# Two chunks per matmul in the last two doubling steps of a block inverse

## The chip, the cores and the metric

The kernel runs on one core of a Trainium2 chip. Its engines work side by side, each through its own instructions in order: TensorE (PE, the matmuls; the loads of its stationary operand are shown apart as PEld), VectorE (DVE), ScalarE (ACT), GpSimd (POOL), and SyncE (SP), which issues the DMAs. The metric is the time of one execution on the device in microseconds (us); less is better.

## What is computed

One inference step of a hybrid decoder layer for a prompt of 2048 tokens and for eight single tokens: a mixer (convolution heads beside gated DeltaNet heads), attention into a memory, and a feed-forward network. The part that matters here is the gated DeltaNet of the prompt, four heads (H) with keys and values of 128 elements. Cut to what matters, the reference says:

```
decay = exp(where(incl, gc[..., :, None] - gc[..., None, :], -inf))
kb = k * beta[..., None]
lower = where(strict, einsum('nbhid,nbhjd->nbhij', kb, k) * decay, 0.0)
a_mat = lower + eye(c)
u = triangular_solve(a_mat, v * beta[..., None], lower=True, unit_diagonal=True)
w = triangular_solve(a_mat, kb * exp(gc)[..., None], lower=True, unit_diagonal=True)
```

For each chunk of tokens a matrix with ones on its diagonal and entries only below it has to be inverted, or a system with it solved. The chunks are then passed through in order, each updating a state of 128x128.

## The kernel before

The kernel takes chunks of 128 tokens (P) and works on blocks of 512 tokens (TB), so a block has four chunks (NT = 4), and there are four blocks (NB). For each block and each head, 16 times in all, `dn_front` (L1810) prepares the four chunks together; `dn_chain` (L1966) then carries the state through them.

`dn_front` is a generator. It builds `lt` (L1822, L1875), the transposed strictly triangular matrices of the four chunks side by side, 128 partitions by 4 x 128. It inverts the 16x16 blocks on the diagonal with small operations of VectorE and GpSimd in `base_inverse` (L1771), whose scratch is the tile `bit` (L1893). The small inverses go through DRAM into two tiles: `Tm` (L1913), the inverse so far, and `W` (L1910), its transpose. Then the inverse is doubled three times, from blocks of 16 to 32, 32 to 64 and 64 to 128 (L1927 to L1961). One doubling fills the off-diagonal block of each pair of finished blocks: the product of the entry below the diagonal with one finished block (`pu1`, result in `u1`, negated), and the product of the other finished block with that (`pu2`). For each of the two products there is one float32 matmul per chunk, four in all. In the first two doublings VectorE multiplies the first product by a mask of -1 and 0 (`nms`, L2114), so that only the wanted blocks stay, and adds the second to `Tm`. Then TensorE transposes `Tm` (`ptw`) and ScalarE copies the result into a new tile `W`. In the third doubling the operands have 64 columns or 64 rows, ScalarE takes both results out of PSUM, and the second goes straight into `W`. At its end `dn_front` hands `W` on.

In profiles the tiles go by their names without numbers: `pu1` and `pu2` both as `pu`, `u1` as `u`. Every instruction has the line L530, where the planner issues it.

The order of the work is planned in two passes. The generators are lanes of `Sched` (L561): the main program emits the projections (`hd`, `glua`, `glub`, then `rg`, `sc`, `fx`, `fy`, `fz`, `dn`), and after each group of matmuls `tick` (L597) lets every lane whose wait is due by a rough clock emit its next operations. All operations go onto a `Tape` (L155). Its `order` (L316) then simulates the five engines with a cost for each operation (L189) and latencies between engines (L159), takes on each engine the ready operation with the lowest key, and so fixes the order in which each engine gets its instructions. It can also move an elementwise operation between VectorE and GpSimd. Operands of the projections are split in two parts (`w`, in float32r) by ScalarE, VectorE and GpSimd.

The tiles of 512 columns come from a pool of 28 (`t2`, L712). A lane asks for room before it takes one. Only one front at a time is in the doublings (`held_l`, L1920), and a front waits for the one before it (L1915).

Of the kernel before, what the change touches and what calls it, by code (L numbers as in the profile page):

```python
# [10 lines left out]
AF = mybir.ActivationFunctionType  # L11
ALU = mybir.AluOpType
AX = mybir.AxisListType

P = 128
# [5 lines left out]
NT = TB // P  # L21
# [91 lines left out]
def elems(ap):  # L113
    n = 1
    for x in ap.shape[1:]:
        n *= x
    return n
# [530 lines left out]
def bc(ap, axis, shape):  # L648
    return ap.unsqueeze(axis).broadcast_to(shape)
# [3 lines left out]
def hybrid_step(ctx: ExitStack, tc: tile.TileContext, i: dict, o: list):  # L653
# [4 lines left out]
    GS, PE, SP = tape.port(nc.gpsimd, "pool"), tape.port(nc.tensor, "pe"), tape.port(nc.sync, "sp")  # L658
    V, A, G = Engine(tape.port(nc.vector, "dve"), "dve", C), Engine(tape.port(nc.scalar, "act"), "act", C), Engine(GS, "pool", C)
    S = Sched(C)  # L660

    def dma(out, in_, after=0.0):
        SP.dma_start(out=out, in_=in_)
        n = 4
        for x in out.shape:
            n *= x
        C.at["sp"] = max(C.at["sp"] + 60, C.when([in_]), after)
        C.at["dma"] = max(C.at["dma"], C.at["sp"] + 1100) + max(n / 360.0, 60.0)
        C.ready[out.name] = max(C.ready.get(out.name, 0.0), C.at["dma"] + 1650)
        C.used[in_.name] = max(C.used.get(in_.name, 0.0), C.at["dma"])  # L670

    def mm(out, lhsT, rhs, start, stop, skip=False):
        n = elems(rhs)
        four = lhsT.dtype == F32 or n < 256
        S.wait(max(C.when([lhsT, rhs]), C.ready.get("free " + out.name, 0.0) if start else 0.0))
        PE.matmul(out, lhsT, rhs, start=start, stop=stop, skip_group_check=skip)
        C.run("pe", 3 + max(n, 64) * (4 if four else 1) / 2.4, [lhsT, rhs], out, 90.0)
# [9 lines left out]
    def transpose(out, in_, identity):  # L687
        S.wait(max(C.when([in_]), C.ready.get("free " + out.name, 0.0)))
        PE.transpose(out, in_, identity)
        C.run("pe", 110.0, [in_], out, 90.0)  # L690
# [14 lines left out]
    def nm(s):  # L705
        uid[0] += 1
        return f"{s}_{uid[0]}"
# [4 lines left out]
    def t2(name, shape=(P, TB), dt=F32):  # L712
        n = 1
        for x in shape[1:]:
            n *= x
        t = t2pool.tile([P, W2], dt, tag="t2", name=nm(name))
        live["t2"].add(t.name)
        assert len(live["t2"]) <= NT2, sorted(live["t2"])
        v = t[: shape[0], :n]
        if len(shape) == 3:  # L720
            v = v.rearrange("p (a b) -> p a b", a=shape[1])
        return v
# [7 lines left out]
    def drop(*tiles):  # L730

        for t in tiles:
            kind = "t2" if t.name in live["t2"] else "act"
            live[kind].remove(t.name)
# [4 lines left out]
    def ps(name, tag="s", shape=(P, TB)):  # L739
        n = 1  # L740
        for x in shape[1:]:
            n *= x
        t = psum.tile([P, 512], F32, tag=tag, name=nm(name), bufs=C.nbank[tag])
        v = t[: shape[0], :n]
        at = C.bank_free(tag)
        C.ready["free " + v.name] = 0.0 if at == float("inf") else at
        C.ring.setdefault(tag, []).append(v.name)
        if len(shape) == 3:
            v = v.rearrange("p (a b) -> p a b", a=shape[1])
        elif len(shape) == 4:  # L750
            v = v.rearrange("p (a b c) -> p a b c", a=shape[1], b=shape[2])
        return v

    def small(name, shape, tag=None, bufs=None, dt=F32):
        return sm.tile(list(shape), dt, tag=tag or name, name=nm(name), bufs=bufs)

    def const(name, shape, dt=F32):
        return cst.tile(list(shape), dt, tag=name, name=name)
# [994 lines left out]
    def z_full(z):  # L1753

        f = z.rearrange("a b -> (a b)").rearrange("(c x) -> c x", c=NT)
        return f[:, 0 : P * P].rearrange("c (r i) -> r c i", i=P)

    def z_diag(z):

        return z[:, 0:2048].rearrange("p (j i) -> p j i", i=P)[:, :, 0:16]  # L1760

    def z_odd(z):

        f = z.rearrange("a b -> (a b)").rearrange("(c x) -> c x", c=NT)
        return f[:, 0 : 64 * P].rearrange("c (r i) -> r c i", i=P)
# [39 lines left out]
    def left(x, s, odd=0):  # L1805
        return x.rearrange("p c (b e s) -> p c b e s", e=2, s=s)[:, :, :, odd, :]

    held_x, held_w, held_l = [], [], []

    def dn_front(h, b, sc, prev, out):  # L1810
# [11 lines left out]
        du, lt = (t2(k, (P, NT, P)) for k in ("du", "lt"))  # L1822
# [19 lines left out]
        for c in range(NT):  # L1842
            V.scalar_tensor_tensor(
                out=du[:, c, :], in0=rb[:, c, :], scalar=gcol[:, c : c + 1], in1=mneg, op0=ALU.subtract, op1=ALU.add
# [30 lines left out]
        for c in range(NT):  # L1875
            V.scalar_tensor_tensor(
                out=lt[:, c, :], in0=pkk[:, c, :], scalar=brk[:, c : c + 1], in1=du[:, c, :], op0=ALU.mult, op1=ALU.mult
# [11 lines left out]
        for c in range(NT):  # L1889
            mm(pqk[:, c, :], kT[:, cs(c)], qT[:, cs(c)], True, True)  # L1890
        V.tensor_tensor(out=at, in0=pqk, in1=du, op=ALU.mult)
        drop(qT, vT)
        bit = t2("bit", (32, 512))  # L1893
        out["pre"] = True
        yield x16

# [6 lines left out]
            out=t16.rearrange("p (i j) -> p i j", j=16), in_=w16[:, 0:256].rearrange("p (j i) -> p i j", i=16), func=AF.Copy  # L1903
        )
        dma(z_odd_diag(zw[z]), w16[1:32:2, 0:256].rearrange("p (j i) -> p j i", i=16))
        dma(z_diag(zt_[z]), t16.rearrange("p (j i) -> p j i", i=16))
        drop(bit, du)
        held_x.pop()
        held_w.pop()
        W = t2("W", (P, NT, P))  # L1910
        GS.memset(W[64:P], 0.0)
        dma(W[0:64], z_odd(zw[z]))
        Tm = t2("Tm", (P, NT, P))  # L1913
        dma(Tm, z_full(zt_[z]))
        yield lambda: prev is None or "done" in prev  # L1915
        yield [Tm, lt, W]

        u1 = u1s[0]
# [3 lines left out]
        lo = small("lo", [P, NT, 64], bufs=1)  # L1922
# [1 line left out]
        yield lo  # L1924


        for s in LEV[:-1]:  # L1927
            n = nms[s].shape[0]
            yield ("ps", "s")
            pu = ps("pu1", shape=(n, NT, 64))  # L1930
            for c in range(NT):
                mm(pu[:, c, :], (lo if n == 64 else lt)[:, c, :], left(Tm, s)[:, c], True, True)
            V.tensor_tensor(out=u1[:n], in0=pu, in1=bc(nms[s], 1, [n, NT, 64]), op=ALU.mult)
            yield u1
            yield ("ps", "s")
            pu = ps("pu2", shape=(P, NT, 64))
            for c in range(NT):
                mm(pu[:, c, :], W[:, c, :], u1[:, c, :], True, True)
            V.tensor_tensor(out=left(Tm, s), in0=pu.rearrange("p c (b s) -> p c b s", s=s), in1=left(Tm, s), op=ALU.add)
            yield Tm  # L1940
            yield ("ps", "s")
            pt = ps("ptw", shape=(P, NT, P))
            for c in range(NT):
                transpose(pt[:, c, :], Tm[:, c, :], ident)
            drop(W)
            W = t2("W", (P, NT, P))
            A.activation(out=W, in_=pt, func=AF.Copy)
            yield W

        held_l.pop()  # L1950
        yield ("ps", "s")
        pu = ps("pu1", shape=(P, NT, 64))
        for c in range(NT):
            mm(pu[64:P, c, :], lt[:, c, 64:P], Tm[:, c, 0:64], True, True)
        A.activation(out=u1[64:P], in_=pu[64:P], func=AF.Copy, scale=-1.0)
        yield u1
        yield ("ps", "s")
        pu = ps("pu2", shape=(64, NT, 64))
        for c in range(NT):
            mm(pu[:, c, :], u1[64:P, c, :], W[64:P, c, 64:P], True, True)  # L1960
        A.activation(out=W[0:64, :, 64:P], in_=pu, func=AF.Copy)  # L1961
        yield W
        drop(lt, Tm)
        out.update(kd=kd, vn=vn, W=W, at=at, qg=qg, kT=kT, s12=s12, brk=brk, held=held, done=True)
# [146 lines left out]
    mneg = const("mneg", [P, P])  # L2111
    GS.memset(mneg, 0.0)
    GS.affine_select(out=mneg, in_=mneg, compare_op=ALU.is_ge, fill=-1e30, base=0, pattern=[[1, P]], channel_multiplier=-1)
    LEV = (16, 32, 64)  # L2114
    nms = {}
    for s, n_ in ((16, 64), (32, P)):
        m = const(f"nms{s}", [n_, 64])
        GS.memset(m, -1.0)
        nb, w_ = 64 // s, n_ // 64 * s
        GS.affine_select(out=m, in_=m, compare_op=ALU.is_ge, fill=0.0, base=s - w_, pattern=[[-w_, nb], [0, s]], channel_multiplier=1)  # L2120
        GS.affine_select(out=m, in_=m, compare_op=ALU.is_ge, fill=0.0, base=w_ - 1, pattern=[[w_, nb], [0, s]], channel_multiplier=-1)
        nms[s] = m
    A.activation(out=nea, in_=nea, func=AF.Exp)
    V.tensor_scalar(out=nea, in0=nea, scalar1=-1.0, scalar2=None, op0=ALU.mult)

# [118 lines left out]
    for pair in PAIRS:  # L2244
# [3 lines left out]
        for st in STEPS:  # L2248
# [49 lines left out]
            if st[0] == "h":  # L2298
                for b in pair:
                    S.add(dn_front(k, b, scs_[b], before(fr_, b, k), fr_[b, k]), SLACK)  # L2300
                    chains.append(S.add(dn_chain(k, b, fr_[b, k], scs_[b], before(ch_, b, k), ch_[b, k]), SLACK))
# [52 lines left out]
    for dh in range(2):  # L2354
        for hp in range(2):
            wts = [ws.get("w_mqT", "r", e, dh * TB) for e in range(4 * hp, 4 * hp + 4)]
            for k in range(4):
                pt = pm("wk")
                for hh in range(2):
                    for c in range(2):  # L2360
                        w_ = wts[2 * hh + c]
# [32 lines left out]
    def square_gemm(w, src, order, xs, done, dec, apart):  # L2394
# [45 lines left out]
        out=sel2, in_=ident.rearrange("p (j c) -> p c j", j=4)[:, 0:DEC, :], op=ALU.add, axis=AX.X  # L2440
# [707 lines left out]
```

## Time and profile before

| | us |
|---|---|
| median of 3 runs | 2921.02 |
| lowest, highest | 2919.77, 2921.06 |
| the profiled execution | 2920.37 |
| its span, first to last instruction | 2918.7 |

The profile is of one execution. It shows for each engine how long it was busy, and groups instructions by engine, operation and tiles; a row of a group ends with its busy time, the mean duration of one instruction in ns, and the idle time of the engine just before them. A table of stretches gives busy time and the number of instructions of each engine between two times, counted from the start of the span. The timeline merges neighbouring instructions of one form; its columns are start, length, engine, line, operation, tiles, form and count. As matmuls overlap, the length of a group there reaches into the next group.

### The profile page before, as it was taken

How to read it: one execution, taken by the hardware profiler on the slowest of the kernel's cores; microseconds unless marked ns; L12 is line 12 of the kernel's file. 1: busy time of each engine (PE TensorE's matmuls, PEld its weight loads, DVE VectorE, ACT ScalarE, POOL GpSimd, SP SyncE). 2: the span in 40 equal slices, each digit the busy share in tenths (PEclk: the TensorE clock that was granted, in tenths of full speed). 3: DMA queues.
4: the chain of work that ended last, by engine and by line, in shares of the span. 5: the costliest groups of instructions: out<-in, count | busy, mean ns of one | idle time of the engine just before them, and what ended most of it. 6: DMA issues, size and time to landing. Idle time of an engine off the chain costs nothing.

```text
span 2918.7 us, 55833 instructions
## 1 busy us (share of the span) xinstructions
PE 2880.8 (99%) x19620; PEld 2599.1 (89%) x19620; DVE 2477.8 (85%) x5383; ACT 1447.7 (50%) x3031; POOL 749.6 (26%) x848
## 2 busy tenths in 40 slices
PE   9999999999989999999999999999999999999998
PEld 7999878888878887999988789999888999999998
DVE  8768998999969977988888977888867888888888
ACT  7544555555764445555555444444444444444444
POOL 3211243443513024622201710000532232400000
PEclk9999999999999999999999999999999999999999
DMA  6433334778764434766677767777626666666664
GB/s 220 146 105 106 119 122 144 235 252 263 231 236 126 124 102 124 258 183 224 209 257 258 257 218 253 244 231 241 201 87 222 208 214 192 210 232 193 214 212 130
DMA packets 363033, 569.41 MB, mean 195 GB/s; under 512 B 55840, under 2 KB 158560, under 8 KB 362736
## 3 DMA queue, kind: packets, MB, share of 16 engines
q1 hardware_dynamic: 362752, 565.84, 60.3%
q8 instruction: 155, 2.54, 0.3%
q14 instruction: 126, 1.03, 0.1%
HBM read 457.77 MB, written 108.51 MB: 194 GB/s over the span
## 4 chain that ended last, share of the span: by engine, by line
PE 86%; DVE 7%; DMA 4%; issue 2%; ACT 1%; POOL 1%; SPq 0%; POOLq 0%; DVEq 0%; ACTq 0%
PE hd L530 12%; PE fy L530 11%; PE rg L530 11%; PE fz L530 8%; PE fx L530 7%; PE dn L530 6%; PE dx L530 5%; PE sc L530 5%; PE glub L530 3%; PE glua L530 3%; PE dz L530 3%; PE pu L530 2%; DVE cacc L530 2%; PE mkv L530 1%; PE dy L530 1%
## 5 line engine op out<-in xcount | busy, mean ns | idle before, releaser
L530 ACT ACTIVATE w<-raw 128x512 fp32r<-128x512 f32 (+1 forms) x1066 | 649.2, 619 | 898.4 <-PE dx L530 131.1
L530 DVE TENSOR_TENSOR w<-raw,w 128x512 fp32r<-128x512 f32 (+1 forms) x866 | 609.1, 708 | 157.3 <-ACT w L530 145.8
L530 PE MATMUL fy<-op,w 128*128 128x256 f32 (+1 forms) x3168 | 434.8, 282 | 0.9 <-DMA w<-sums 0.7
L530 PEld LDWEIGHTS fy<-op,w 128*128 128x128 f32 x3168 | 399.3, 188 | 6.7 <-DVE ffs L530 2.2
L530 PE MATMUL hd<-hT,w 128*128 128x512 f32 (+2 forms) x1920 | 395.6, 356 | 1.3 <-ACT w L530 1.2
L530 POOL TENSOR_TENSOR w<-raw,w 128x512 fp32r<-128x512 f32 (+1 forms) x200 | 281.2, 1412 | 372.7 <-ACT w L530 323.0
L530 DVE SCALAR_TENSOR_TENSOR cacc<-cu,cw,cacc 128x512 f32<-128x512 f32 x480 | 358.7, 747 | 8.6 <-ACT cacc L530 4.8
L530 PEld LDWEIGHTS hd<-hT,w 128*128 128x128 f32 x1920 | 302.4, 188 | 45.8 <-ACT w L530 1.8
L530 PE MATMUL fx<-op,w 128*128 128x256 f32 (+1 forms) x2112 | 297.2, 283 | 0.3 <-ACT ffs L530 0.2
L530 PE MATMUL fz<-op,w 128*128 128x256 f32 (+1 forms) x2112 | 285.0, 282 | 1.7 <-DMA w<-sums 1.0
L530 PEld LDWEIGHTS fx<-op,w 128*128 128x128 f32 x2112 | 269.5, 189 | 6.7 <-issue 2.6
L530 PEld LDWEIGHTS fz<-op,w 128*128 128x128 f32 x2112 | 264.1, 188 | 6.1 <-issue 2.6
L530 PE MATMUL dx<-fo,w 128*128 128x256 f32 (+1 forms) x1344 | 198.3, 283 | 2.3 <-DVE x L530 2.3
L530 PE MATMUL rg<-pT,w 128*128 128x512 f32 x768 | 190.7, 400 | 1.6 <-ACT pr L530 1.4
L530 PE MATMUL dn<-ff,w 128*128 128x512 f32 (+2 forms) x960 | 191.8, 352 | 0.0
L530 PE MATMUL sc<-w,hT 128*128 128x512 f32 x768 | 189.2, 401 | 1.0 <-ACT pr L530 1.0
L530 PE MATMUL rg<-catS,w 128*128 128x512 f32 (+2 forms) x960 | 186.8, 352 | 0.0
L530 PEld LDWEIGHTS dx<-fo,w 128*128 128x128 f32 x1344 | 174.7, 188 | 5.8 <-DVE x L530 4.4
L530 PEld LDWEIGHTS rg<-catS,w 128*128 128x128 f32 x960 | 154.5, 188 | 24.6
L530 PEld LDWEIGHTS sc<-w,hT 128*128 128x128 f32 x768 | 142.2, 189 | 34.1 <-ACT pr L530 2.7
L530 PEld LDWEIGHTS rg<-pT,w 128*128 128x128 f32 x768 | 140.9, 188 | 34.6 <-ACT pr L530 2.9
L530 PEld LDWEIGHTS dn<-ff,w 128*128 128x128 f32 x960 | 151.1, 188 | 20.9
(423 smaller groups left out, 4847.2 us busy)
## 6 DMA issues: line engine op xcount, KB each, us to landing
w<-sums SPq DMA_DIRECT2D x222, 512.0 KB, 4.3
raw<-in_w_gate_dram SPq DMA_DIRECT2D x192, 256.0 KB, 3.4
sums<-w SPq DMA_DIRECT2D x66, 512.0 KB, 4.1
raw<-in_w_up_dram SPq DMA_DIRECT2D x118, 256.0 KB, 3.6
raw<-in_w_down_dram SPq DMA_DIRECT2D x224, 128.0 KB, 2.9
raw<-in_w_in_dram SPq DMA_DIRECT2D x96, 256.0 KB, 3.1
raw<-sums SPq DMA_DIRECT2D x74, 256.0 KB, 3.2
raw<-wk SPq DMA_DIRECT2D x64, 256.0 KB, 2.8
```

Of the source, the lines that this page charges most:

```text
L530: fn(*args, **kw)
```

## The change

The doubling from 16 to 32 keeps its form. For the two later ones two chunks, an even one and the odd one after it, share one matmul: their operands are put as two blocks of a block-diagonal operand, so that there are two matmuls per product in place of four, all with 128 rows and 128 columns in the stationary operand.

For the step 32 to 64 the entries below the diagonal of both chunks are copied by ScalarE into `lp`, which is the small tile `lo` in another shape and is cleared by GpSimd first; the finished blocks of the odd chunk are copied into places of the even chunk in `Tm` and `W` that are still unused. The first product is taken out of PSUM by ScalarE with the factor -1, without a mask. The four off-diagonal results go from PSUM into `Tm` by four copies of ScalarE. For the step 64 to 128 the same is done in `lt` and `u1` (as `ud`), with two clears by GpSimd in each, and the results are copied into `W` in two parts.

`renew` transposes `Tm` as before but writes into the same tile `W`. The scratch of `base_inverse` lies in the first 32 partitions of `Tm`, which is taken earlier for this; `bit` is gone. One mask, `nms`, is left.

```diff
--- before.py
+++ after.py
@@ -1890,7 +1890,8 @@
             mm(pqk[:, c, :], kT[:, cs(c)], qT[:, cs(c)], True, True)
         V.tensor_tensor(out=at, in0=pqk, in1=du, op=ALU.mult)
         drop(qT, vT)
-        bit = t2("bit", (32, 512))
+        Tm = t2("Tm", (P, NT, P))
+        bit = Tm[0:32].rearrange("p c x -> p (c x)")
         out["pre"] = True
         yield x16
 
@@ -1904,13 +1905,12 @@
         )
         dma(z_odd_diag(zw[z]), w16[1:32:2, 0:256].rearrange("p (j i) -> p j i", i=16))
         dma(z_diag(zt_[z]), t16.rearrange("p (j i) -> p j i", i=16))
-        drop(bit, du)
+        drop(du)
         held_x.pop()
         held_w.pop()
         W = t2("W", (P, NT, P))
         GS.memset(W[64:P], 0.0)
         dma(W[0:64], z_odd(zw[z]))
-        Tm = t2("Tm", (P, NT, P))
         dma(Tm, z_full(zt_[z]))
         yield lambda: prev is None or "done" in prev
         yield [Tm, lt, W]
@@ -1924,41 +1924,86 @@
         yield lo
 
 
-        for s in LEV[:-1]:
-            n = nms[s].shape[0]
-            yield ("ps", "s")
-            pu = ps("pu1", shape=(n, NT, 64))
-            for c in range(NT):
-                mm(pu[:, c, :], (lo if n == 64 else lt)[:, c, :], left(Tm, s)[:, c], True, True)
-            V.tensor_tensor(out=u1[:n], in0=pu, in1=bc(nms[s], 1, [n, NT, 64]), op=ALU.mult)
-            yield u1
-            yield ("ps", "s")
-            pu = ps("pu2", shape=(P, NT, 64))
-            for c in range(NT):
-                mm(pu[:, c, :], W[:, c, :], u1[:, c, :], True, True)
-            V.tensor_tensor(out=left(Tm, s), in0=pu.rearrange("p c (b s) -> p c b s", s=s), in1=left(Tm, s), op=ALU.add)
-            yield Tm
+        def turned(pu):
+            return pu.rearrange("p c (b s) -> p c b s", s=16)
+
+        def renew():
             yield ("ps", "s")
             pt = ps("ptw", shape=(P, NT, P))
             for c in range(NT):
                 transpose(pt[:, c, :], Tm[:, c, :], ident)
-            drop(W)
-            W = t2("W", (P, NT, P))
             A.activation(out=W, in_=pt, func=AF.Copy)
             yield W
 
-        held_l.pop()
+        def copy(out, in_, scale=1.0):
+            A.activation(out=out, in_=in_, func=AF.Copy, scale=scale)
+
         yield ("ps", "s")
-        pu = ps("pu1", shape=(P, NT, 64))
+        pu = ps("pu1", shape=(64, NT, 64))
         for c in range(NT):
-            mm(pu[64:P, c, :], lt[:, c, 64:P], Tm[:, c, 0:64], True, True)
-        A.activation(out=u1[64:P], in_=pu[64:P], func=AF.Copy, scale=-1.0)
+            mm(pu[:, c, :], lo[:, c, :], left(Tm, 16)[:, c], True, True)
+        V.tensor_tensor(out=u1[:64], in0=pu, in1=bc(nms, 1, [64, NT, 64]), op=ALU.mult)
         yield u1
         yield ("ps", "s")
-        pu = ps("pu2", shape=(64, NT, 64))
+        pu = ps("pu2", shape=(P, NT, 64))
         for c in range(NT):
-            mm(pu[:, c, :], u1[64:P, c, :], W[64:P, c, 64:P], True, True)
-        A.activation(out=W[0:64, :, 64:P], in_=pu, func=AF.Copy)
+            mm(pu[:, c, :], W[:, c, :], u1[:, c, :], True, True)
+        V.tensor_tensor(out=left(Tm, 16), in0=turned(pu), in1=left(Tm, 16), op=ALU.add)
+
+        lp = lo.rearrange("p c x -> p (c x)").rearrange("p (g x) -> p g x", g=2)
+        GS.memset(lp, 0.0)
+        for r in (0, 64):
+            up, dn = slice(r, r + 32), slice(r + 32, r + 64)
+            copy(lp[up, :, dn], lt[up, 0:NT:2, dn])
+            copy(lp[dn, :, up], lt[up, 1:NT:2, dn])
+        yield Tm
+        yield from renew()
+        for r in (0, 64):
+            up, dn = slice(r, r + 32), slice(r + 32, r + 64)
+            copy(Tm[dn, 0:NT:2, up], Tm[up, 1:NT:2, up])
+            copy(W[up, 0:NT:2, up], W[dn, 1:NT:2, dn])
+        yield [Tm, lo]
+        yield ("ps", "s")
+        pu = ps("pu1", shape=(P, 2, 64))
+        for g in range(2):
+            mm(pu[:, g, :], lp[:, g, :], left(Tm, 32)[:, 2 * g], True, True)
+        copy(u1[:, 0:2, :], pu, -1.0)
+        yield [u1, W]
+        yield ("ps", "s")
+        pu = ps("pu2", shape=(P, 2, 64))
+        for g in range(2):
+            mm(pu[:, g, :], W[:, 2 * g, :], u1[:, g, :], True, True)
+        for r in (0, 64):
+            up, dn, x = slice(r, r + 32), slice(r + 32, r + 64), slice(r // 2, r // 2 + 32)
+            copy(Tm[dn, 0:NT:2, up], pu[dn, :, x])
+            copy(Tm[dn, 1:NT:2, up], pu[up, :, x])
+        held_l.pop()
+
+        up, dn = slice(0, 64), slice(64, P)
+        GS.memset(lt[up, 0:NT:2, up], 0.0)
+        GS.memset(lt[dn, 0:NT:2, dn], 0.0)
+        copy(lt[dn, 0:NT:2, up], lt[up, 1:NT:2, dn])
+        yield Tm
+        yield from renew()
+        copy(Tm[dn, 0:NT:2, up], Tm[up, 1:NT:2, up])
+        copy(W[up, 0:NT:2, dn], W[dn, 1:NT:2, dn])
+        ud = u1.rearrange("p c x -> p (c x)").rearrange("p (g x) -> p g x", g=2)
+        GS.memset(ud[up, :, up], 0.0)
+        GS.memset(ud[dn, :, dn], 0.0)
+        yield [Tm, lt]
+        yield ("ps", "s")
+        pu = ps("pu1", shape=(P, 2, 64))
+        for g in range(2):
+            mm(pu[:, g, :], lt[:, 2 * g, :], Tm[:, 2 * g, 0:64], True, True)
+        copy(ud[dn, :, up], pu[dn], -1.0)
+        copy(ud[up, :, dn], pu[up], -1.0)
+        yield [u1, W]
+        yield ("ps", "s")
+        pu = ps("pu2", shape=(P, 2, 64))
+        for g in range(2):
+            mm(pu[:, g, :], ud[:, g, :], W[:, 2 * g, dn], True, True)
+        copy(W[up, 0:NT:2, dn], pu[up])
+        copy(W[up, 1:NT:2, dn], pu[dn])
         yield W
         drop(lt, Tm)
         out.update(kd=kd, vn=vn, W=W, at=at, qg=qg, kT=kT, s12=s12, brk=brk, held=held, done=True)
@@ -2111,15 +2156,10 @@
     mneg = const("mneg", [P, P])
     GS.memset(mneg, 0.0)
     GS.affine_select(out=mneg, in_=mneg, compare_op=ALU.is_ge, fill=-1e30, base=0, pattern=[[1, P]], channel_multiplier=-1)
-    LEV = (16, 32, 64)
-    nms = {}
-    for s, n_ in ((16, 64), (32, P)):
-        m = const(f"nms{s}", [n_, 64])
-        GS.memset(m, -1.0)
-        nb, w_ = 64 // s, n_ // 64 * s
-        GS.affine_select(out=m, in_=m, compare_op=ALU.is_ge, fill=0.0, base=s - w_, pattern=[[-w_, nb], [0, s]], channel_multiplier=1)
-        GS.affine_select(out=m, in_=m, compare_op=ALU.is_ge, fill=0.0, base=w_ - 1, pattern=[[w_, nb], [0, s]], channel_multiplier=-1)
-        nms[s] = m
+    nms = const("nms", [64, 64])
+    GS.memset(nms, -1.0)
+    GS.affine_select(out=nms, in_=nms, compare_op=ALU.is_ge, fill=0.0, base=0, pattern=[[-16, 4], [0, 16]], channel_multiplier=1)
+    GS.affine_select(out=nms, in_=nms, compare_op=ALU.is_ge, fill=0.0, base=15, pattern=[[16, 4], [0, 16]], channel_multiplier=-1)
     A.activation(out=nea, in_=nea, func=AF.Exp)
     V.tensor_scalar(out=nea, in0=nea, scalar1=-1.0, scalar2=None, op0=ALU.mult)
 
```

## The prediction

> **What bounds the kernel now.** I read the page first, for which engine fills the span, then the table of stretches, for where that fails.
>
> ```profile
> span 2918.7 us, 55833 instructions
> PE 2880.8 (99%) x19620; PEld 2599.1 (89%) x19620; DVE 2477.8 (85%) x5383; ACT 1447.7 (50%) x3031; POOL 749.6 (26%) x848
> PE 86%; DVE 7%; DMA 4%; issue 2%; ACT 1%; POOL 1%; SPq 0%; POOLq 0%; DVEq 0%; ACTq 0%
> ```
>
> TensorE (PE) is busy for 99% of the span and is 86% of the chain that ended last. All its idle time is 2918.7 - 2880.8 = 37.9 us. So a microsecond of matmul slots taken out is worth nearly a microsecond, wherever nothing else is late. Where something else is late:
>
> ```profile
> core 0: us, PE busy (x) PEld busy (x) DVE busy (x) ACT busy (x) POOL busy (x), PEclk, DMA share, GB/s
> 365.00:438.00 73.00, 69.74 (x378) 51.91 (x377) 66.48 (x156) 39.64 (x88) 31.66 (x52) 0.95 0.40 123
> 584.00:657.00 73.00, 73.00 (x357) 60.06 (x356) 69.19 (x137) 38.16 (x71) 29.92 (x33) 1.00 0.74 251
> 803.00:876.00 73.00, 65.30 (x434) 57.93 (x433) 48.63 (x86) 49.02 (x113) 9.89 (x13) 0.98 0.69 234
> 876.00:949.00 73.00, 70.50 (x476) 63.33 (x475) 67.29 (x162) 35.69 (x92) 27.07 (x36) 0.98 0.44 128
> by line: DVE cacc L530 18.4%; PE rg L530 13.8%; DVE w L530 8.7%; PE sc L530 7.6%; issue 7.0%; PE vp L530 5.6%; DMA vp<-jn 5.3%; DMA catT<-zd 4.3%; PE pu L530 2.1%; DVE tbd L530 2.0%; DVE x L530 1.8%; DVE mx L530 1.8%; DVE dn L530 1.8%; DVE
> ```
>
> At 584 to 657 us PE has no idle time at all, although VectorE (DVE) is busy 95% of it. The exception is 803 to 949 us: PE idles 7.7 + 2.5 = 10.2 us there, and the last row, the chain of waits cut to 800 to 960 us, has DVE's convolution sums (cacc) and weight splits (w) in front. There PE waits for others.
>
> **What the removed matmuls cost.** One float32 matmul is two instructions in the trace. The old steps 32 to 64 and 64 to 128 are, per front, four groups of x8. The timeline of PE gives a group's slot as the distance from its start to the next group's start:
>
> ```profile
> 149.79 3.11 PE L530 MATMUL hd<-hT,w 128*128 128x256 f32 x24
> 152.74 1.00 PE L530 MATMUL pu<-Tm,lt 128*128 128x64 f32 x8
> 153.54 3.83 PE L530 MATMUL hd<-hT,w 128*128 128x256 f32 x27
> 162.99 0.60 PE L530 MATMUL ptw<-ident,Tm 128*128 128x128 f32 x4
> 163.35 0.97 PE L530 MATMUL hd<-hT,w 128*128 128x256 f32 x6
> 167.02 0.68 PE L530 MATMUL pu<-Tm,lt 128*64 128x64 f32 x8
> 167.63 3.13 PE L530 MATMUL hd<-hT,w 128*128 128x256 f32 x24
> 170.69 0.68 PE L530 MATMUL pu<-W,u 64*64 64x64 f32 x8
> 171.29 0.94 PE L530 MATMUL pqk<-qTd,kT 128*128 128x128 f32 x6
> 1469.66 1.58 PE L530 MATMUL fy<-op,w 128*128 128x256 f32 x12
> 1471.07 1.57 PE L530 MATMUL fx<-op,w 128*128 128x256 f32 x12
> ```
>
> A full-width group of 8 takes 153.54 - 152.74 = 0.80 us, a 64-column group 167.63 - 167.02 = 0.61 (the 64*64 one 0.60), a full-width group of 4 (the transposes) 163.35 - 162.99 = 0.36. A group also disturbs its neighbours. Undisturbed, 12 matmuls of 128x256 take 1471.07 - 1469.66 = 1.41 us, so 24 take 2.82. Between full-width groups 24 took 152.74 - 149.79 = 2.95, that is 0.13 more; between 64-column groups 170.69 - 167.63 = 3.06, 0.24 more. I add that edge once per group: 0.93 us for a full-width 8, 0.85 for a 64-column 8, and 0.49 for a full-width 4.
>
> Per front, step 32 to 64 goes from two full-width 8s to two full-width 4s: 2 x (0.93 - 0.49) = 0.88 us. Step 64 to 128 goes from two 64-column 8s to two full-width 4s: 2 x (0.85 - 0.49) = 0.72 us. Step 16 to 32 and both transposes stay as they are. The sum is 1.60 us a front, and the number of fronts is in the counts of `lo`, which each front reads with one group of 8 (columns of the first two rows: PE, its loads, ACT):
>
> ```profile
> 0.00:850.00 850.00, 7.00 (x80) 5.48 (x80) 4.11 (x10) 0.99 0.57 182
> 850.00:2919.00 2069.00, 4.01 (x48) 3.24 (x48) 2.48 (x6) 1.00 0.62 201
> L530 PE MATMUL pu<-u,W 128*128 128x64 f32 x256 | 32.3, 268 | 0.0
> L530 PE MATMUL pu<-Tm,lt 128*128 128x64 f32 (+1 forms) x256 | 27.0, 248 | 0.9 <-DVE at L530 0.9
> L530 PE MATMUL ptw<-ident,Tm 128*128 128x128 f32 x128 | 19.7, 273 | 0.2 <-DVE Tm L530 0.2
> L530 PE MATMUL pu<-Tm,lo 128*64 128x64 f32 x128 | 11.0, 228 | 1.2 <-DMA Tm<-zt 0.7 <-DVE zd L530 0.4 <-issue 0.2
> ```
>
> Ten fronts before 850 us and six after: **PE loses 16 x 1.60 = 25.6 us of slots**, 16.0 of them before 850.
>
> **The weak half of that sum** is step 64 to 128. Inside a group the starts lie (0.68 - 0.23) / 7 = 0.064 us apart for 64 columns and (1.00 - 0.27) / 7 = 0.104 for 128, with 0.23 and 0.27 the means of one matmul in the rows above. Half as many, nearly twice as dear: the inside of a group saves only 8 x 0.064 - 4 x 0.104 = 0.10 us, and the rest of the 0.72 is edge. The Trainium skill, "TensorE: Matmul & The Clock Gate", section "LDWEIGHTS (loading the stationary operand)", says that a weight load costs its columns, whatever the rows: by that rule step 64 to 128 would save nothing, and the sum would be 16 x 0.88 = 14.1 us. The trace nearly agrees inside the group and disagrees at its edges. For the edges the skill's "TensorEngine Tiling (Array Packing)", section "Key Properties", has a reason: a change of tiling mode drains TensorE, and the new full-width groups would not change it. I keep the edge, since two stretches of the same 24 matmuls show it.
>
> **What is added beside PE.** On ScalarE (ACT) a front gains 20 copies and loses 2:
>
> ```profile
> L530 ACT ACTIVATE bds<-pbt 128x64 f32<-128x64 f32 x4 | 0.9, 216 | 2.1 <-PE pbt L530 2.1
> L530 ACT ACTIVATE wbd<-wraw 128x64 fp32r<-128x64 f32 x1 | 0.2, 248 | 0.0
> L530 ACT ACTIVATE oh<-sel 16x128 fp32r<-16x128 f32 x8 | 2.4, 302 | 4.5 <-PE pdd L530 4.5
> L530 ACT ACTIVATE chj<-pk 128x128 bf16<-128x128 f32 x64 | 16.7, 276 | 8.5 <-PE pk L530 7.2 <-DVE dn L530 1.0
> L530 ACT ACTIVATE u<-pu 64x256 f32<-64x256 f32 x16 | 6.1, 380 | 13.2 <-PE pu L530 12.9
> L530 POOL MEMSET W<- 64x512 f32 x16 | 8.4, 523 | 83.2 <-issue 47.8 <-DVE sqj L530 15.7 <-ACT chj L530 6.4
> L530 DVE TENSOR_TENSOR Tm<-pu,Tm 128x256 f32<-128x256 f32 x32 | 13.3, 417 | 4.0 <-PE pu L530 3.8
> ```
>
> Eight of 64 elements within SBUF at 0.248 us, four of 64 from PSUM at 0.216, three of 128 within SBUF at 0.302 and five of 128 from PSUM at 0.276 make 5.1 us. Less two of 64x256 at 0.38, ACT gains 4.4 us a front, 70 us in all, and goes from 50% to 52% of the span. What it delays is weight splits, which run ahead of PE. GpSimd (POOL) gains five memsets; at no more than the 0.52 us of the row they are 2.6 us a front, 42 in all, on an engine 26% busy. DVE loses two operations of 128x256 at 0.42 us, 0.83 a front and 13.3 in all, 8.3 of them before 850. Renewing the transpose in place waits for the reads that its input waited for already: nothing. Scratch in the result's tile frees at the same point as its own tile did, and the load into it comes after the scratch is read, through two DMAs as before: nothing. No DMA is added or moved.
>
> **New waits.** Five groups of a front now wait for ACT copies: the first of step 32 to 64 for two copies within Tm and four into lp, its second for one PSUM copy and two within W, the transposes behind it for four PSUM copies, and the two groups of step 64 to 128 for two copies each. That makes 80 places. Behind a waiting group stand, in order on PE, the hd or fy matmuls of the projection. In the old groups PE idled 0.9 + 0.2 + 1.2 = 2.3 us over 112 groups (the last four rows of the fence on counts), 0.02 us each, because the planner puts a group where it expects its input. I take 0.025 us: 2 us. Lower bound: nothing, since a later group only leaves its place to an hd or fy matmul. Upper bound: the longest of these strings bare at every place, four PSUM copies of 0.216 us less the 0.42 us of the DVE operation that they replace, 80 x 0.44 = 35 us. The near row is the 0.02. On ACT and POOL the copies and memsets wait for PE to have read `lo` or `u1`; behind them stand weight splits, for which PE waits in turn. The cover is that ACT and POOL stand idle for 50% and 74% of the span; without it the cost is again that of the upper bound.
>
> **Given back at 803 to 949.** PE arrives there 16.0 us earlier, DVE with only 8.3 us less work. If DVE sets that stretch alone, 7.7 us come back; if PE does, none. PE is busy 93% of it and DVE leads its chain, so I take half, 3.9 us.
>
> **The sum:** 25.6 - 2.0 - 3.9 = 19.7 us off the profiled execution's 2920.4 (span 2918.7 and 1.7 around it), which lies 0.7 us below the median 2921.0: **2901 us**.
>
> **The rivals.**
> 1. *PE sets everything*: no hand-off costs, and DVE's relief carries 803 to 949 along. 2920.4 - 25.6 = 2895 us. For it: the 0.02 us a group; against it: the 10.2 us of idle time there.
> 2. *Width costs what count saves*: step 64 to 128 gains only the inside of its groups, 0.2 us a front. 16 x 1.08 = 17.3, less the same 5.9: 2909 us. For it: 0.064 against 0.104; against it: the 0.24 us edge. The skill's LDWEIGHTS rule points this way.
> 3. *The stretch at 803 does not move*: whatever PE gains before it (16.0 us) turns into idle time there, and the planner's new order costs 4 us more of idle time elsewhere. 25.6 - 20 = 5.6 us: 2915 to 2920. For it: DMA and ACT steps in that chain, which the change leaves alone.
> 4. *Slower: PE stands at the ACT copies.* The place is the transposes behind the four PSUM copies, and the groups behind two copies. PE issues in order, so a late copy holds the hd or fy matmuls behind the group too. It decides from (25.6 + 5.8) / 80 = 0.39 us a place; at the upper bound of 0.44 the time is 2920.4 - 25.6 + 35 = 2930. Against it: ACT is half idle.
>
> **How the numbers follow.** Forecast (2897 to 2907) 0.50, rival 1 (2890 to 2897) 0.20, rival 2 (2907 to 2914) 0.10, rival 3 0.12, rival 4 0.08. A measurement of this kernel can tell 0.2%, 5.8 us, from no change. Faster: 0.50 + 0.20 + 0.10 = 0.80; same 0.12; slower 0.08. Rivals 3 and 4 lie outside the range, which runs from 2890 (all of the slots and a little of the 37.9 us of idle time) to 2914.
>
> **What would show it.** Right: pu<-Tm,lt and the new step groups as x4 in 0.36 to 0.40 us; hd stretches of 24 beside them at 2.95 instead of 3.06 us; 512 fewer PE instructions counting loads; PE still 99%; ACT near 1515 us. Rival 2: hd stretches still 3.06. Rival 3: idle time at 803 to 949 grown from 10 towards 26 us. Rival 4: PE pu or ptw waiting for ACT in tenths of a microsecond, many times. The forecast fails if the edge is not the group's own, or if the new order opens an idle stretch long enough to lower the granted clock, as at 365 to 438 us (0.95).

## The result and the profile after

The changed kernel takes 2913.43 us (median of 8 runs, 2907.88 to 2915.49) against 2921.39 for the kernel before beside it (8 runs, 2919.77 to 2924.88): a ratio of 0.9965, 95% interval 0.9956 to 0.9974. That is 8 us gained where the prediction said 20; the time lies in the range, 0.6 us below its upper end. The page of after, its span, busy times and chain:

```profile
span 2911.7 us, 55716 instructions
PE 2863.9 (98%) x19364; PEld 2590.6 (89%) x19364; DVE 2452.5 (84%) x5317; ACT 1506.4 (52%) x3310; POOL 807.4 (28%) x959
PE 87%; DVE 5%; DMA 4%; ACT 2%; issue 1%; POOL 1%; SPq 0%; POOLq 0%; DVEq 0%; ACTq 0%
```

PE's busy time fell by 16.9 us, not 25.6, and its idle time rose from 37.9 to 2911.7 - 2863.9 = 47.8 us. The rows of PE's groups by form, and stretches of its timeline in block 0 (its columns are as before):

```profile
L530 PE MATMUL pu<-u,W 128*128 128x64 f32 x192 | 26.0, 272 | 0.7 <-issue 0.6
L530 PE MATMUL ptw<-ident,Tm 128*128 128x128 f32 x128 | 19.9, 277 | 0.2 <-ACT Tm L530 0.2
L530 PE MATMUL pu<-Tm,lt 128*128 128x64 f32 x64 | 9.4, 271 | 0.0
L530 PE MATMUL pu<-W,u 128*128 128x64 f32 x64 | 9.0, 261 | 0.2 <-issue 0.2
L530 PE MATMUL pu<-Tm,lo 128*128 128x64 f32 x64 | 8.9, 262 | 0.0
```

```profile
176.83 0.55 PE L530 MATMUL pu<-Tm,lt 128*128 128x64 f32 x4
177.19 3.13 PE L530 MATMUL hd<-hT,w 128*128 128x256 f32 x24
180.16 0.55 PE L530 MATMUL pu<-W,u 128*128 128x64 f32 x4
180.52 3.11 PE L530 MATMUL hd<-hT,w 128*128 128x256 f32 x24
183.47 0.38 PE L530 MATMUL pch<-S,kT 128*128 128x128 f32 x2
```

The new groups do what was forecast: a group of 4 takes 177.19 - 176.83 = 0.36 us, the 24 hd matmuls behind it 180.16 - 177.19 = 2.97 and 183.47 - 180.52 = 2.95 us, and in the groups' rows PE waits for ACT's new copies 0.2 us in all. So the slots went, and the copies don't hold PE. Where the time came back shows one row, 1100 to 1500 us, in the table of stretches of before (first) and of after (second), and in the longest waits of PE in that stretch in after (us in total, times, longest):

```profile
1100.00:1500.00 400.00, 396.32 (x2723) 358.41 (x2722) 348.82 (x687) 212.09 (x488) 140.49 (x144) 1.00 0.64 207
```

```profile
1100.00:1500.00 400.00, 386.86 (x2642) 352.86 (x2641) 363.30 (x689) 225.00 (x553) 174.51 (x195) 0.97 0.65 212
```

```profile
PE rg L530 <- ACT pT L530: 4.9, 1, 4.9
PE fy L530 <- DVE ffs L530: 4.1, 1, 4.1
PE pu L530 <- DMA Tm<-zt: 2.7, 1, 2.7
```

PE idles 13.1 us there instead of 3.7, and its mean granted clock fell from 1.00 to 0.97: with each of these three waits come 6.83 us at half speed (the clock records of the trace). At 803 to 949 us, where the prediction put its loss, idle time fell:

```profile
803.00:876.00 73.00, 69.17 (x479) 62.75 (x478) 50.65 (x102) 53.62 (x126) 9.67 (x21) 0.98 0.69 221
876.00:949.00 73.00, 73.00 (x425) 62.09 (x424) 52.18 (x135) 36.04 (x97) 14.81 (x22) 1.00 0.40 120
```

It is 3.8 us now, against 10.2 before.

**An account of the span.** For the experiments I split each span by the start times of its matmuls. *Fronts* is what the groups `pu` and `ptw` cost: each instruction at the median distance to the next start that its form has in before, plus what they and the matmuls just ahead of them take beyond it (the edges). *Gaps* is the sum of all starts that come over 0.4 us later than that median. *Half speed* is the excess in stretches whose clock is recorded as 0.5. *Rest* is the excess of all other matmuls. The remainder, 2725 us of slots outside the fronts, is the same in every kernel here, and some 8 us lie at the span's ends.

| profiled execution | span | fronts | gaps | half speed | rest |
|---|---|---|---|---|---|
| before | 2918.7 | 85.8 | 48.3 | 6.1 | 45.2 |
| after | 2911.7 | 61.3 | 59.9 | 15.1 | 41.6 |

The fronts lost 24.5 us (the prediction: 25.6). Gaps gave 11.6 back, half speed 9.0; the rest lost 3.6. So the question is where the 20 us of gaps and half speed come from.

### The profile page after: what moved, and what is told of

Read it like the earlier page. It is cut to its first block, busy times and chain, and to the rows that moved or that the text cites. A ratio compares the mean times of both kernels' runs of the same rounds, so it can differ in the third digit from the quotient of the medians.

```text
span 2911.7 us, 55716 instructions
## 1 busy us (share of the span) xinstructions
PE 2863.9 (98%) x19364; PEld 2590.6 (89%) x19364; DVE 2452.5 (84%) x5317; ACT 1506.4 (52%) x3310; POOL 807.4 (28%) x959
## 4 chain that ended last, share of the span: by engine, by line
PE 87%; DVE 5%; DMA 4%; ACT 2%; issue 1%; POOL 1%; SPq 0%; POOLq 0%; DVEq 0%; ACTq 0%
PE fy L530 12%; PE rg L530 11%; PE hd L530 11%; PE fz L530 8%; PE fx L530 8%; PE dn L530 6%; PE sc L530 6%; PE dx L530 5%; PE glua L530 3%; PE glub L530 3%; PE dz L530 3%; PE pu L530 2%; PE mkv L530 1%; DMA w<-sums 1%; PE pch L530 1%
## 5 line engine op out<-in xcount | busy, mean ns | idle before, releaser
L530 DVE TENSOR_TENSOR w<-raw,w 128x512 fp32r<-128x512 f32 (+1 forms) x847 | 599.2, 711 | 174.4 <-ACT w L530 169.8
L530 POOL TENSOR_TENSOR w<-raw,w 128x512 fp32r<-128x512 f32 (+1 forms) x219 | 304.8, 1396 | 325.2 <-ACT w L530 243.2
L530 PEld LDWEIGHTS rg<-catS,w 128*128 128x128 f32 x960 | 154.2, 188 | 25.2 <-issue 0.9
```

Source lines behind the costliest of these rows:

```text
L530: fn(*args, **kw)
```

## The experiments

Four theories were held in turn. *Theory 1*: the planner's order is chance, and this one is a poor draw. *Theory 2*: the change's own copies and clears cost it, by holding GpSimd's queue (2a), by the scratch in `Tm` that delays the load into it (2b), or by a longer way of each front (2c). *Theory 3*: between 1100 and 1500 us other engines end last, so that freed PE time turns into gaps whatever frees it. *Theory 4*, formed after the first eleven runs: Theory 1, but for the planner's first pass, which puts the fronts' matmuls among the projections'. Ratios are to the kernel before on the same chip.

**The planner's second pass.** Two constants were altered, one in each pair of runs, in before and in after:

```diff
-        "dve": dict(pe=149, dve=127, act=128, pool=155, sp=120),
-        "act": dict(pe=164, dve=142, act=150, pool=170, sp=145),
+        "dve": dict(pe=151, dve=129, act=130, pool=157, sp=120),
+        "act": dict(pe=166, dve=144, act=152, pool=172, sp=145),
```

```diff
-BACKLOG = 1800
+BACKLOG = 1850
```

> The kernel before, planned again: the planner's latencies from VectorE and ScalarE to every engine are 2 ns longer; no operation changes. Theory 1 (the slots were saved, and the planner's new order gave most of it back by chance): the order alone moves a time by several microseconds, so this lies 4 to 12 us from 2921, more likely above it, with PE idle time of 40 to 55 us in place of 37.9. Theory 2 (the new ScalarE copies and GpSimd clears themselves make PE wait): orders hardly matter, this lies within 3 us of 2921.

> The changed kernel, planned again in the same way (2 ns). Theory 1: 4 to 15 us from 2913, more likely below it (2898 to 2909), with other idle stretches of PE than the three around 1133, 1238 and 1455 us. Theory 2: within 3 us of 2913, and PE idle time of 47.8 us as before in stretches around the fronts.

> The kernel before, planned again: the threshold from which elementwise work moves from VectorE to GpSimd is 1850 in place of 1800. Theory 1: 4 to 12 us from 2921. Theory 2: within 3 us of 2921.

> The changed kernel with the same threshold of 1850. Theory 1: 4 to 15 us from 2913, and over the three orders of each kernel the changed one is 15 to 22 us faster on the mean. Theory 2: within 3 us of 2913, and 8 us faster than the kernel before on the mean.

| | median us | ratio, 95% interval | gaps | half speed |
|---|---|---|---|---|
| before, latencies | 2924.39 | 1.0005 (0.9996 to 1.0015) | 53.1 | 3.2 |
| after, latencies | 2914.34 | 0.9971 (0.9959 to 0.9983) | 58.3 | 13.3 |
| before, backlog | 2915.88 | 0.9982 (0.9972 to 0.9992) | 47.7 | 6.3 |
| after, backlog | 2914.27 | 0.9974 (0.9964 to 0.9983) | 61.2 | 10.3 |

Before moves by 8 us with its order. After doesn't: three orders lie within a microsecond, with the same three waits (with the other backlog `fy` is 2.7 us and one of 3.5 us for `ffu` comes to them). By this Theory 1 seemed to fall. What I overlooked is that both constants belong to the second pass, and the order in which PE's matmuls are emitted is made by the first. The traces show how little these runs redraw it. Count, for each of the 128 transposes `ptw` of the fronts, the matmuls of the projections `hd` to `dn` that start before it: 128 of 128 have the same count in after and in after with other latencies, 116 with the other backlog, and 112 and 108 in the two pairs of before; between before and after it is 20.

**One step alone.** Each of the two paired steps without the other; the step left out has its form of before, with its mask or its half-width matmuls. For 64 to 128 alone the core of the edit to after is:

```diff
-        for g in range(2):
-            mm(pu[:, g, :], lp[:, g, :], left(Tm, 32)[:, 2 * g], True, True)
-        copy(u1[:, 0:2, :], pu, -1.0)
...
+        for c in range(NT):
+            mm(pu[:, c, :], lt[:, c, :], left(Tm, 32)[:, c], True, True)
+        V.tensor_tensor(out=u1, in0=pu, in1=bc(nms32, 1, [P, NT, 64]), op=ALU.mult)
```

> Only the step from 32 to 64 in the new form; the step from 64 to 128 is that of the kernel before. By the slots it saves 16 x 0.88 = 14.1 us of PE: 2907 if nothing is given back. Theory 2c: thirteen copies of the twenty are in this step, so most is given back here: 2914 to 2919.

> Only the step from 64 to 128 in the new form; the step from 32 to 64 is that of the kernel before (eight matmuls, mask and sum on VectorE). By the slots it saves 16 x 0.72 = 11.5 us of PE. Theory 2c: only seven copies and four clears a front are left, less is given back: 2908 to 2914. If the edge of a 64-column group is not its own (rival 2 of the prediction): 16 x 0.2 = 3 us, 2918.

| | median us | ratio, 95% interval | fronts | gaps | half speed |
|---|---|---|---|---|---|
| 32 to 64 alone | 2919.10 | 0.9990 (0.9981 to 0.9999) | 72.4 | 56.8 | 4.7 |
| 64 to 128 alone | 2922.07 | 1.0003 (0.9994 to 1.0012) | 78.1 | 61.0 | 1.9 |

The slots go in both: 13.4 us of fronts in the first (the prediction's term: 14.1), 7.7 in the second (11.5). In the second some 6.9 of the 7.7 lie at edges and 0.8 inside groups. But gaps grow by 8.5 and 12.7 us, as if either half brought the whole of them. No sum of parts does that. The first time is at the upper edge of what Theory 2c allowed (2919), the second 8 us above it (2914).

**The clears and the scratch.** The five clears done by ScalarE, as a copy times zero, and the scratch of `base_inverse` in a tile of its own again:

```diff
-        GS.memset(lp, 0.0)
+        copy(lp, lt[:, 0:2, :], 0.0)
...
-        GS.memset(lt[up, 0:NT:2, up], 0.0)
+        copy(lt[up, 0:NT:2, up], lt[up, 0:NT:2, up], 0.0)
```

```diff
-        Tm = t2("Tm", (P, NT, P))
-        bit = Tm[0:32].rearrange("p c x -> p (c x)")
+        bit = t2("bit", (32, 512))
```

> The changed kernel with its five clears per front made by ScalarE (a copy with the factor 0) in place of GpSimd. Theory 2a (the clears stand at the head of GpSimd's queue until PE has read the old contents, and hold the splits behind them): 4 to 10 us faster than 2913, PE idle time under 42 us. Theory 2c (it is the longer way of a front through ScalarE copies that makes the last fronts late): no gain or 1 to 4 us slower, since ScalarE gets five more copies a front. Theory 1 (chance of the order): anywhere within 8 us of 2913.

> The changed kernel with the scratch of the base inverse in a tile of its own again, as before the change. Theory 2b (scratch in the result's tile makes the load into it late): the waits of PE for the load of Tm (3.1 us) go, 3 to 8 us faster than 2913. Theories 2a and 2c: within 3 us of 2913.

The clears on ScalarE give 2923.31 us (1.0007, 0.9998 to 1.0015), the own scratch 2920.29 (0.9994, 0.9986 to 1.0003): both slower than after, with gaps of 68.7 and 62.1 us, and both outside all that was expected. Nothing got better where 2a or 2b put the cost: PE's wait for the load of `Tm` fell from 3.1 to 1.0 us, and the time rose. So neither is shown to be what is missing. The own scratch keeps the order of after (112 of the 128 transposes at their place, the waits of 4.9 and 4.0 us again) and is still 7 us slower; why, no run shows.

**Slots without copies, copies without slots.** First before with the two wide steps done for two chunks only, at the PE groups of after; then after without its copies within SBUF and three clears; then after with every paired matmul issued twice. The cores of the three edits:

```diff
-            for c in range(NT):
-                mm(pu[:, c, :], W[:, c, :], u1[:, c, :], True, True)
...
+            for c in range(NT // k):
+                mm(pu[:, c, :], W[:, k * c, :], u1[:, c, :], True, True)
```

```diff
-        GS.memset(lp, 0.0)
...
-            copy(lp[up, :, dn], lt[up, 0:NT:2, dn])
-            copy(lp[dn, :, up], lt[up, 1:NT:2, dn])
...
-            copy(Tm[dn, 0:NT:2, up], Tm[up, 1:NT:2, up])
-            copy(W[up, 0:NT:2, up], W[dn, 1:NT:2, dn])
```

```diff
-        for g in range(2):
+        for g in (0, 1, 0, 1):
             mm(pu[:, g, :], lp[:, g, :], left(Tm, 32)[:, 2 * g], True, True)
```

> The kernel before with the two wide steps done for two of the four chunks only: the steps 32 to 64 and 64 to 128 of the other two chunks are left out, so the output is not the reference's. PE's groups are those of the change (x4, full width, 16 fronts), with none of its copies within SBUF, none of its clears, and no copies from PSUM beyond the two of before. Theory 2 (the copies and clears cost what is missing): without them the whole 24 to 26 us of slots show, 2895 to 2902 us. Theory 3 (exposure: between 1100 and 1500 us other engines end last, and PE time freed ahead of it or in it turns into idle gaps and half-speed clock there, whatever replaces the matmuls): 2908 to 2916 us, PE idle time over 44 us in the profiled execution (before: 37.9) and the half-speed stretches at 1100 to 1500 us again.

> The changed kernel without its 11 copies within SBUF a front and without three of its five clears (lp and the two of lt), so the two chunks of a pair are no longer put block diagonal and the output is not the reference's; the groups of PE and the copies from PSUM stay. Theory 2: 2898 to 2906 us, since most of what the moves cost goes. Theory 3: 2909 to 2917 us, as the changed kernel, with the same idle gaps between 1100 and 1500 us.

> The changed kernel with each matmul of the paired groups issued twice into the same place (same result): the four groups of a front are x8 again, all full width, 16 x 4 x 0.44 = 28 us of slots more than the changed kernel; all copies and clears stay. Theory 2 (copies and clears cost some 16 us wherever they are): 2936 to 2944 us. Theory 3 (the freed slots were only worth their 8 us, because others end last in a part of the span): 2919 to 2928 us, PE idle time back at 36 to 41 us and fewer half-speed stretches between 1100 and 1500 us.

| | median us | ratio, 95% interval | fronts | gaps | half speed |
|---|---|---|---|---|---|
| half the steps | 2929.03 | 1.0021 (1.0011 to 1.0030) | 61.5 | 67.8 | 25.2 |
| no moves | 2915.70 | 0.9981 (0.9972 to 0.9990) | 63.0 | 68.3 | 4.8 |
| twice | 2941.76 | 1.0070 (1.0057 to 1.0083) | 91.0 | 62.6 | 8.8 |

These three left neither theory standing. (`k` is 1 in the step 16 to 32 and 2 in the next.) Without the moves the time stays, as Theory 3 said, so they are not what is missing, unless the new order of this kernel hides their cost. Matmuls put back cost 2941.76 - 2913.43 = 28.3 us for 28 us of slots, the full price: that is in Theory 2's range, where Theory 3 allowed 6 to 15. And the kernel with less work than both, no copy added and 24 us of slots gone, is slower than before: Theory 2 had it at 2895 to 2902 us, Theory 3 at 2908 to 2916. PE's longest waits in it:

```profile
PE lnp L530 <- DMA lnx<-cvT: 8.1, 2, 7.8
PE vp L530 <- ACT jn L530: 3.4, 3, 1.9
PE pkt L530 <- ACT chj L530: 2.9, 1, 2.9
PE pkt L530 <- DVE lnx L530: 2.6, 1, 2.6
```

These are other places than in after: a transpose (`lnp`) of the convolution's branch stands on PE ahead of its data, 7.8 us long. What eight edits have in common, whatever they add or take, is gaps of 57 to 69 us, where the three orders of before have 48 to 53. All but the own scratch put the fronts elsewhere: at most 40 of the 128 transposes keep the place that they have in before or in after. That led to Theory 4.

**Another draw of the first pass.** One constant in the price list of the rough clock:

```diff
-                ns = 80 + 0.86 * n + 93 * (len(ins) - 1) + (60 if kw.get("accum_out") is not None else 0)
+                ns = 96 + 0.86 * n + 93 * (len(ins) - 1) + (60 if kw.get("accum_out") is not None else 0)
```

> The changed kernel with one constant altered: the price of a ScalarE operation in the first stage of the planner, where the matmuls of the fronts are put among those of the projections, is 96 + 0.86 n instead of 80 + 0.86 n. The work is the same, instruction for instruction; only the order of all engines differs. The price was picked out of some twenty for which the planner's own account leaves PE idle least (23 us, against 31 for the changed kernel and 32 for the kernel before). Theory 2 and Theory 3 (what is missing belongs to the change, to its added operations or to what the freed slots uncover): 2910 to 2917 us, as all three orders of the changed kernel that ran. Theory 4 (what is missing is the first stage's order, which every edit of the kernel redraws, and of which the kernel before has a good draw): the loss beyond the slots falls back to that of the kernel before, 105 to 110 us instead of 125, and the time is 2897 to 2906 us, with no PE idle gap over 3 us between 1100 and 1500 us.

The time is 2903.31 us (5 runs, 2902.07 to 2909.08), ratio 0.9945, 95% interval 0.9931 to 0.9958. The interval of after (0.9956 to 0.9974) just touches it, those of the other two orders of after lie above it. That is 6 us less than after by the ratios, and 11 by the medians against the kernel before beside each, with the same work. Of the 128 transposes 56 keep the place that they have in after. Its page, its stretch from 1100 to 1500 us and PE's longest waits in that stretch:

```profile
span 2900.4 us, 55726 instructions
PE 2856.6 (98%) x19364; PEld 2583.1 (89%) x19364; DVE 2462.8 (85%) x5319; ACT 1510.2 (52%) x3313; POOL 810.3 (28%) x957
```

```profile
1100.00:1500.00 400.00, 388.20 (x2704) 354.43 (x2703) 360.38 (x686) 230.17 (x559) 170.47 (x190) 0.99 0.66 218
```

```profile
PE fy L530 <- DVE ffs L530: 5.0, 1, 5.0
PE pu L530 <- DMA Tm<-zt: 2.3, 2, 2.0
PE pod L530 <- ACT osc L530: 2.0, 1, 2.0
```

By the account: fronts 61.9, gaps 57.0, half speed 3.9, rest 44.2. The time came out as Theory 4 said, and not as 2 or 3 did. Two of its details were wrong: one wait of 5.0 us stays between 1100 and 1500 us, and gaps and half speed and rest sum to 105.1 plus the ends' 8, 113 where 105 to 110 was said. Of the 11.3 us between the spans of after and of this kernel 11.2 are half speed (gaps lost 2.9, the rest gained 2.6): before the last microseconds of the span after has seven half-speed stretches, 34 us, and this kernel two, 10 us. The mean granted clock of the single runs says the same: 0.992 to 0.994 in all eight of after, 0.995 to 0.997 in all five of this kernel. So the other order took away the half speed. It didn't take away the idle time between 1100 and 1500 us: that is still 400 - 388.2 = 11.8 us, against 13.1 in after and 3.7 in before.

## Why the prediction was right, and where it was wrong

**The slots: right.** 24.5 us against 25.6. The paired matmuls had their full price when put back (28.3 us for 28). The weak half was weaker than taken: step 64 to 128 alone gave 7.7 us, 0.48 a front in place of 0.72. Step 32 to 64 alone gave 13.4, and both together 3.4 more than their sum.

**Inside and edge: right in kind.** The prediction's 0.10 us a group makes 3.2 us inside the 32 groups of step 64 to 128, and leaves 8.3 of the 11.5 to edges; alone the step gave some 0.8 and 6.9. The Trainium skill's rule, "TensorE: Matmul & The Clock Gate", section "LDWEIGHTS (loading the stationary operand)", that a load costs its columns, by which the inside saves nothing, is near the 0.8 and says nothing of the 6.9 us at edges. Rival 2 put the step at 0.2 us a front; the 0.48 lies midway between that and the 0.72. Its sign, `hd` stretches still at 3.06 us, didn't come (2.97 and 2.95). Its time (2907 to 2914) holds the result, but by chance: the slots that it doubted are 1.1 us off in all.

**New waits: right.** PE waited 0.2 us for the copies at the groups shown; the term was 2.0. ACT is busy 1506.4 us, where 1515 was promised, and 256 matmuls and as many loads are gone. Rival 4 falls by the 0.2 us; leaving out 11 of a front's copies and three clears gained nothing either.

**The give-back: wrong.** This is the step that failed: "Given back at 803 to 949", 3.9 us. There nothing came back (idle 10.2 to 3.8 us), so rival 3 has the wrong place too, though its size (20 us) is near and its smaller term, 4 us of idle time from the planner's new order, is of the kind that the runs show. Elsewhere gaps and half speed grew by 11.6 + 9.0 = 20.6 us, five times the term. The largest gaps are four single waits that end at 716, 1133, 1238 and 1456 us, 5.1 + 4.9 + 4.1 + 2.7 = 16.8 us, and with them come 24 of the 34 us at half speed. The prediction took the order of before as given and let the work slide along it. The change redraws the order: the fronts' matmuls come at other places among the projections (108 of the 128 transposes), and PE, which goes in order, meets operations that stand behind others on ACT or DVE. At 1126 us the timelines of PE (first) and ACT of after show one such:

```profile
1127.34 0.60 PE L530 MATMUL ppt<-ident,pr 128*128 128x128 f32 x4
1132.85 1.22 PE L530 MATMUL rg<-pT,w 128*128 128x512 f32 x2 [4.91 <-ACT pT L530]
```

```profile
1130.11 0.63 ACT L530 ACTIVATE op<-tt 128x512 fp32r<-128x512 f32 x1 [0.51 <-DVE tt L530]
1131.68 0.63 ACT L530 ACTIVATE op<-tt 128x512 fp32r<-128x512 f32 x1 [0.94 <-POOL tt L530]
1132.22 1.06 ACT L530 ACTIVATE pT<-ppt 128x512 fp32r<-128x512 f32 x2
```

The transposes were issued from 1127.34; their copy out of PSUM (`pT`) waits until 1132.22 behind operations of the feed-forward part (`op<-tt`), which wait in turn for DVE and GpSimd. With the other price PE has no such wait there, and the time, 2903 us, lies within the 2897 to 2907 of the forecast. The prediction's last sentence named this way to fail, "if the new order opens an idle stretch long enough to lower the granted clock", but gave it no price and no chance. That the time still lies in the range, by 0.6 us, is luck: a term of 3.9 us was off by 17, and only the width of the range held it.

**What stays open.** The order alone is worth 6 to 11 us with the same work, nearly all of it half speed: that is shown. That the order of before is a good draw is only a conclusion from the gaps of nine edited kernels (57 to 69 us) beside its own; before was not run with another price of the first pass. With the other price the gaps of after stay 8.7 us above those of before (57.0 against 48.3), and whether they belong to the order or to the change isn't settled. Against the draw speaks the row from 1100 to 1500 us: PE idles 3.7 to 5.3 us there in the three orders of before, and 9.3 to 18.2 us in every other kernel here, whatever its edit and its order. So a form of Theory 3, for this stretch alone, isn't excluded. The other price was picked for after, out of some twenty by the planner's own account of PE's idle time, and the 12.6 us between it and the best order of before that ran (2915.88) may be nearer the change's worth than the 18.

## What to carry to other kernels

Where a planner or a greedy schedule sets the order, an edit is two changes: its slots, which can be summed from the profile, and a new draw of the order, which here moved the time of the same matmuls by 8 us in before and by 6 to 11 us in after. Measure the edit over several orders, and shake the pass that sets the order of the bounding engine, not only the last one, before calling a gain or a loss the edit's own. Read a loss by single long waits first: each of them can also cost clock.

## What the runs showed of the hardware

**The clock can halve after short waits.** PE's timeline of after, and the table of stretches just behind it (the 0.50 is the granted clock):

```profile
427.83 0.37 PE L530 MATMUL pg<-g,um 128*128 128x16 f32 x2 [1.82 <-DVE g L530]
428.05 0.37 PE L530 MATMUL pg<-g,ones 128*128 128x16 f32 x2
```

```profile
428.40:431.70 3.30, 3.30 (x11) 2.77 (x11) 2.57 (x10) 1.88 (x7) 2.35 (x2) 0.50 0.97 322
```

An idle time of 1.82 us was followed by 3.41 us at half speed; the waits of 4.9, 4.1 and 2.7 us came with 6.83 each. Length alone doesn't decide: a wait of 2.8 us in the kernel with the other price had none. Its row among the longest waits:

```profile
PE sc L530 <- ACT pr L530: 3.8, 2, 2.8
```

Nor does it take a long wait: in before, the half-speed stretch that the prediction points at (365 to 438 us) began after 3.4 us in which PE idled 0.45 us in all:

```profile
397.10:400.50 3.40, 2.95 (x24) 2.70 (x24) 3.40 (x10) 2.67 (x5) 2.08 (x5) 1.00 0.19 41
400.60:407.30 6.70, 5.87 (x16) 2.36 (x16) 6.54 (x24) 1.63 (x5) 4.26 (x13) 0.50 0.11 39
```

What decides it these runs don't show. The Trainium skill, "TensorE: Matmul & The Clock Gate", section "HAM oscillation — how this bites in real kernels", puts the limit at idle gaps of over some 3.4 us; here half speed followed one of 1.82 us, and the trace differs.

**One VectorE operation took 5.04 us** where its group's mean is 0.71, in the DVE and POOL timelines of after:

```profile
709.00 5.04 DVE L530 TENSOR_TENSOR w<-raw,w 128x512 fp32r<-128x512 f32 x1
```

```profile
708.50 1.26 POOL L530 TENSOR_TENSOR catS<-cat,catS 128x512 fp32r<-128x512 f32 x1
709.71 0.11 POOL L530 MEMSET w<- 32x16 f32 x1
709.77 1.28 POOL L530 TENSOR_TENSOR catS<-cat,catS 128x512 fp32r<-128x512 f32 x1
711.02 2.47 POOL L530 TENSOR_TENSOR w<-raw,w 128x512 fp32r<-128x512 f32 x2
713.44 0.30 POOL L530 MEMSET lo<- 128x256 f32 x1
```

It began in the middle of a two-input operation of GpSimd and ended at 714.04 us, 0.55 us after the last of four, which had one memset of 0.11 us between them. Behind it on DVE stood `chr`, for which PE waited until 716 us, its longest wait in after:

```profile
PE pch L530 <- DVE chr L530: 6.3, 4, 5.1
```

The Trainium skill, "SBUF — State Buffer", section "Terms", says that the two engines share a port pair, and the loser is blocked for a whole instruction; the trace fits a loss against four.
